# First layer's channel gate: four modulation slabs on VectorE in place of TensorE

## The chip, the cores and the metric

The kernel runs on one core of a Trainium2 chip. TensorE (PE in the profile) multiplies matrices into PSUM, VectorE (DVE) and ScalarE (ACT) work on rows of 128 partitions, GpSimd (POOL) does elementwise work between SBUF tiles, and SyncE (SP) issues the DMAs. The metric is the device time of one execution in microseconds. The kernel before takes 2351.58 us, the median of three runs (2349.04 to 2352.13).

## The reference

Two layers work on 512 latent and 256 context tokens of width 1024. Each layer has a token-mixing part (a convolution branch and differential attention, merged by gates, then one output projection) and a channel part (a squared-ReLU MLP of width 4096, called mixing below, with weights `w_mlp1` and `w_mlp2`). Both parts are modulated by vectors computed from a condition:

```
mx = silu(c) @ w_ada[i] + b_ada[i]            # for the latent tokens
mc = silu(c_ctx) @ w_ada[i] + b_ada[i]        # for the context tokens
shift1, scale1, gate1, shift2, scale2, gate2 = split(mx, 6)     # and the same of mc
h = rmsnorm(x, norm1_g) * (1 + scale1) + shift1
x = x + gate1 * token_mixing(h)
h = rmsnorm(x, norm2_g) * (1 + scale2) + shift2
x = x + gate2 * (square(relu(h @ w_mlp1)) @ w_mlp2)
```

`w_ada[i]` is 1024 by 6144. In the first layer both token groups go through all of this; in the last layer only the latent tokens do. Only the last value in the list, `gate2` of the first layer, is touched by the change. It is first used when the products with `w_mlp2` are added to `x`.

## The kernel before, in words

**Numbers.** Almost every product is made of three: each operand is split into a high half (rounded, made on ScalarE, L76) and a low half (the rest, made on VectorE or GpSimd, L77), and `mm3` adds high by high, high by low and low by high (L109 to L111). A block is 24 such products into one PSUM bank, 512 latent columns wide, or 256 wide for the context tokens and for halves of the latent tokens. Latent blocks have two banks (`mm_tile`), the others two (`mc`). Weights are loaded in slabs of 1 MB through `load_slab` into a ring of two raw tiles and split there; within the first layer's mixing part the low halves are made on GpSimd.

**Slabs.** The modulation weights of a layer are cut into 24 slabs of 256 columns, four for each of the six vectors. Slabs 20 to 23 are `gate2`. There are two ways to work on a slab.

`ada_slab` (L217) uses TensorE: it loads the slab through the raw ring (L81), runs eight products in plain float32 with the two condition vectors as weights (L224; the profile shows 16 instructions), copies the result on ScalarE (L230), makes two transposes on TensorE (L233), and on VectorE two reductions and an addition (L236, L239). The first layer's 24 slabs all go this way: eight at the start, eight among the merge gates, four in the attention output projection (products `ya`) and slabs 20 to 23 in the conv output projection (products `yc`, L1114 and L1115).

`ada_rows` (L245) uses VectorE, and does all 24 slabs of the second layer while the first layer's mixing part runs. It is a generator. A step is half a slab: a load of 512 KB into a tile of its own, `araw`, of which there is one (L263), then for four rows of 128 inputs and the two conditions one multiply-add into `adaac` (L279; the very first of each condition is a product on ScalarE, L276). At the end of a step the next half is loaded. The step after a slab's second half begins by closing that slab: a 32 by 32 block transpose (L289) and a reduction (L290) into `adp`. After eight slabs a fold on TensorE (L252, eight instructions) sums over partitions, and an addition on VectorE (L254) writes the values of these slabs.

**What sets the order.** The engines' order is worked out when the program is built, by a scheduler that goes by readiness in a simulated timeline and by program order. An instruction sits in its engine's queue at the place found then; if what it needs is late on the chip, all behind it on that engine waits. A step is taken at a *tick*, a call of `ada_step` (L1219), whose VectorE instructions may not be placed before the last one recorded in `state["done"]`, a residual addition (L1154) or the low half of a hidden value (L1235).

**The order of the work around the change.** In the first layer: `ya` products, then `yc` products with the low half `cl` (L1103) of the convolution's output, then the output projection `o` (`out_slabs` with a norm: four slabs; the first two go over the two latent halves and the context one after another, two blocks for each; the last two go together, for the first latent half, then the second, then the context, and each is followed by `norm2`), then mixing in four chunks `cch`. In a chunk the hidden blocks `f` (w1, four slabs of two blocks for each token group) are followed by the blocks `r` (w2, four slabs, latent m 0 and 1, then context m 0 and 1). The last chunk's `r` blocks go over the halves, as in the output projection, with the next layer's norm behind them.

Ticks before: in the hidden blocks after each latent block but the last of the chunk, which gives 3 in chunk 0 (its first two slabs go over halves and have none) and 7 in each of chunks 1 to 3; in the `r` blocks of chunks 0 to 2 after each latent block, 8 each. That is 3 + 21 + 24 = 48 ticks for 48 steps. After the hidden blocks of chunk 3, `drain` finishes what is left: the last slab's close and the last fold.

Of the kernel before, what the change touches and what calls it, by code (L numbers as in the profile page):

```python
# [14 lines left out]
P = 128  # L15
# [36 lines left out]
def trunk_kernel(  # L52
# [192 lines left out]
    def ada_rows(i, L):  # L245
# [3 lines left out]
        def fold(s0):  # L249
            ps = state["mi"](f"adaps{i}_{s0}")  # L250
            for c_ in range(4):
                nc.tensor.matmul(ps[32 * c_ : 32 * c_ + 32, :32], fold32, part[:, c_],  # L252
                                 start=True, stop=True, tile_position=(0, 32 * c_))
            nc.vector.tensor_tensor(  # L254
                out=L["ad"][:, :, 2 * s0 : 2 * s0 + 16].rearrange("p q (n m) -> p n q m", n=8),
                in0=ps[:, :32].rearrange("p (n q m) -> p n q m", n=8, q=2),
                in1=L["cols"][:, R_BADA + 2 * s0 : R_BADA + 2 * s0 + 16]
                .rearrange("p (n m) -> p n m", n=8).unsqueeze(2).to_broadcast([P, 8, 2, 2]),
                op=ALU.add)

        def load(n):
            r = state["rp"].tile([P, KT // 2, 256], F32, tag="araw", bufs=1, name=f"ar{i}_{n}")
            nc.sync.dma_start(r, rows(w_ada[i], 256 * (n // 2), 256)[:, 4 * (n % 2) : 4 * (n % 2) + 4])  # L263
            return r

        r = load(0)
        for n in range(48):
            s = n // 2
            if n % 2 == 0:
                a = state["tp"].tile([P, 512], F32, tag="t2k", bufs=state["nt"], name=f"adaac{i}_{s}")  # L270
                a = a.rearrange("p (q n) -> p q n", q=2)
            for j in range(4):
                k = 4 * (n % 2) + j
# [8 lines left out]
            if n < 47:  # L282
                r = load(n + 1)
            yield
            if n % 2:
                if s % 8 == 0:
                    part = spool.tile([P, 4, P], F32, tag="dg", bufs=1, name=f"adp{i}_{s}")[:, :, :32]
                b = state["tp"].tile([P, 512], F32, tag="t2k", bufs=state["nt"], name=f"adat{i}_{s}")
                nc.vector.transpose(out=b, in_=a.rearrange("p q n -> p (q n)"))  # L289
                nc.vector.tensor_reduce(  # L290
                    out=part[:, :, 4 * (s % 8) : 4 * (s % 8) + 4].rearrange("p c n -> p n c"),
                    in_=b.rearrange("p (n c r) -> p n c r", n=4, c=4), axis=AX.X, op=ALU.add)
                if s % 8 == 7:
                    fold(s - 7)
# [154 lines left out]
    for i in range(DEPTH):  # L449
# [658 lines left out]
        for s in range(2):  # L1108
# [89 lines left out]

        w1 = {}
# [188 lines left out]
```

## Time and profile before

| | |
|---|---|
| median of three runs | 2351.58 us |
| the profiled execution | 2353.61 us, with a span of 2351.8 us |
| TensorE busy | 2276.6 us, 97% |
| VectorE busy | 1476.0 us, 63% |
| ScalarE busy | 995.2 us, 42% |
| GpSimd busy | 687.3 us, 29% |
| mean granted TensorE clock | 0.988 |

How to read it: times in rows of the timeline are microseconds from the start of the span, then the duration, the engine, the line of the kernel, the instruction, what it writes and from what, and how many were put together in the row; a bracket holds the idle time of the engine before it and what ended that. Rows of the waits give who waited for whom, the sum, the number of times and the longest. A matmul row of TensorE is longer than the distance to the next one, since products are pipelined: the distance between starts is what a product costs.

| place in the first layer | us from the start |
|---|---|
| last `ya` product | 712.37 |
| first `yc` product | 714.45 |
| first `o` product | 751.81 |
| first `r` residual | 901.9 |
| last fold | 1300.8 |

### The profile page before, as it was taken

The page shows a single profiled execution, that of the slowest core. Times are in us where ns is not written, and L with a number is a line of the kernel's source. Part 1 is how long each engine was busy: PE and PEld are TensorE (multiplying, and loading weights), DVE is VectorE, ACT ScalarE, POOL GpSimd, SP SyncE. Part 2 cuts the span into 40 slices and gives each one's busy share as a digit, 9 for nine tenths or more (in the row PEclk, how much of TensorE's full clock was granted, in tenths as well). Part 3 has the DMA queues.
Part 4 walks back from the last instruction along what each step waited for, and adds up shares of the span by engine and source line. Part 5 has one row for each costly group of instructions (what it writes and reads, how often), then busy time and mean ns, then how long its engine had stood idle before and what let it go on. Part 6 is the DMA issues. An engine that isn't in the chain of part 4 may idle for free.

```text
span 2351.8 us, 36393 instructions
## 1 busy us (share of the span) xinstructions
PE 2276.6 (97%) x14626; PEld 2042.8 (87%) x14626; DVE 1476.0 (63%) x2587; ACT 995.2 (42%) x1965; POOL 687.3 (29%) x790
## 2 busy tenths in 40 slices
PE   7999999999999999999999999999899999999999
PEld 6999998888888988888888988999877879888887
DVE  6777776699656455565655465767759966433332
ACT  5556654522332362332415255655542334432432
POOL 1866764100000133232223266757610000000000
PEclk9999999999999999999999999999999999999999
DMA  9111111143535124333343211111114323223222
GB/s 313 57 42 34 44 46 44 46 160 125 180 119 175 51 81 127 115 128 115 113 130 127 89 46 57 44 43 44 61 59 141 112 90 126 90 90 98 99 90 72
DMA packets 222570, 224.76 MB, mean 96 GB/s; under 512 B 6256, under 2 KB 212544, under 8 KB 222272
## 3 DMA queue, kind: packets, MB, share of 16 engines
q1 hardware_dynamic: 222400, 222.43, 29.4%
q8 instruction: 115, 1.88, 0.3%
q14 instruction: 55, 0.45, 0.1%
HBM read 208.73 MB, written 13.67 MB: 95 GB/s over the span
## 4 chain that ended last, share of the span: by engine, by line
PE 83%; DVE 7%; ACT 4%; POOL 2%; DMA 2%; issue 1%; SPq 0%; ACTq 0%; POOLq 0%; DVEq 0%
PE r L109 6%; PE r L110 6%; PE r L111 6%; PE f L110 6%; PE f L109 6%; PE f L111 6%; PE gt L109 3%; PE gt L110 3%; PE gt L111 3%; PE qk L109 2%; PE qk L110 2%; PE qk L111 2%; PE v L109 2%; PE v L110 2%; PE v L111 2%; PE o L109 2%
## 5 line engine op out<-in xcount | busy, mean ns | idle before, releaser
L110 PE MATMUL f<-h2l,h_w 128*128 128x512 f32 (+1 forms) x832 | 284.5, 343 | 1.1 <-POOL h2l L77 1.1
L109 PE MATMUL f<-h2h,h_w 128*128 128x512 f32 (+1 forms) x832 | 282.9, 343 | 2.2 <-ACT h2h L76 1.7
L111 PE MATMUL f<-h2h,l_w 128*128 128x512 f32 (+1 forms) x832 | 283.0, 342 | 0.0
L109 PE MATMUL r<-fh,h_w 128*128 128x512 f32 (+1 forms) x832 | 283.0, 341 | 0.0
L110 PE MATMUL r<-fl,h_w 128*128 128x512 f32 (+1 forms) x832 | 282.9, 340 | 0.0
L111 PE MATMUL r<-fh,l_w 128*128 128x512 f32 (+1 forms) x832 | 282.8, 340 | 0.0
L77 POOL TENSOR_TENSOR l_w<-r_w,h_w 128x1024 fp32r<-128x1024 f32 x64 | 157.8, 2487 | 339.5 <-ACT h_w L76 339.5
L76 ACT ACTIVATE h_w<-r_w 128x1024 fp32r<-128x1024 f32 x128 | 128.6, 1052 | 254.3 <-PE r L110 117.2
L959 DVE SCALAR_TENSOR_TENSOR cacc<-z,cols,cacc 128x783 f32<-128x783 f32 (+1 forms) x240 | 201.2, 891 | 0.3
L279 DVE SCALAR_TENSOR_TENSOR adaac<-ar,cvec,adaac 128x256 f32<-128x256 f32 x336 | 160.8, 541 | 44.6 <-DMA ar<-in_w_ada_dram 22.7
L109 PE MATMUL qk<-h_wqk,h1h 128*128 128x256 f32 x640 | 183.3, 289 | 0.7 <-ACT h1h L76 0.7
L1154 DVE SCALAR_TENSOR_TENSOR X<-r,ad,X 128x512 f32<-128x512 f32 (+1 forms) x104 | 65.1, 625 | 189.0 <-PE r L111 188.8
L110 PE MATMUL qk<-l_wqk,h1h 128*128 128x256 f32 x640 | 180.6, 284 | 0.0
L111 PE MATMUL qk<-h_wqk,h1l 128*128 128x256 f32 x640 | 176.9, 285 | 0.3 <-POOL h1l L77 0.3
L726 DVE TENSOR_REDUCE st<-S 128x1 f32<-128x768 f32 (+1 forms) x160 | 134.7, 846 | 66.8 <-PE S L724 65.3
L109 PEld LDWEIGHTS f<-h2h,h_w 128*128 128x128 f32 x832 | 158.1, 191 | 21.1 <-ACT h2h L76 2.3
L110 PEld LDWEIGHTS f<-h2l,h_w 128*128 128x128 f32 x832 | 159.1, 191 | 19.6 <-POOL h2l L77 1.9
L111 PEld LDWEIGHTS f<-h2h,l_w 128*128 128x128 f32 x832 | 158.8, 191 | 17.7
L111 PEld LDWEIGHTS r<-fh,l_w 128*128 128x128 f32 x832 | 157.7, 190 | 17.7
L109 PEld LDWEIGHTS r<-fh,h_w 128*128 128x128 f32 x832 | 157.7, 190 | 17.4
L110 PEld LDWEIGHTS r<-fl,h_w 128*128 128x128 f32 x832 | 157.8, 190 | 17.2
L1235 DVE TENSOR_TENSOR fl<-fr,fh 128x512 fp32r<-128x512 f32 (+1 forms) x104 | 67.9, 659 | 138.4 <-ACT fr L1234 138.2
(255 smaller groups left out, 6297.7 us busy)
## 6 DMA issues: line engine op xcount, KB each, us to landing
r_w<-in_w_mlp_dram SPq DMA_DIRECT2D x64, 1024.0 KB, 5.4
ada<-in_w_ada_dram SPq DMA_DIRECT2D x24, 1024.0 KB, 6.1
ar<-in_w_ada_dram SPq DMA_DIRECT2D x48, 512.0 KB, 3.5
r_wqk<-in_w_in_dram SPq DMA_DIRECT2D x32, 512.0 KB, 5.1
r_wg<-in_w_in_dram SPq DMA_DIRECT2D x16, 1024.0 KB, 5.9
r_wv<-in_w_in_dram SPq DMA_DIRECT2D x8, 1024.0 KB, 5.2
r_wao<-in_w_attn_out_dram SPq DMA_DIRECT2D x8, 1024.0 KB, 4.8
r_wo<-in_w_out_dram SPq DMA_DIRECT2D x8, 1024.0 KB, 7.3
```

The costliest lines, as they stand in the source:

```text
L76: nc.scalar.activation(out=hi, in_=src, func=AF.Copy)
L77: return (lo_eng or nc.vector).tensor_tensor(out=lo, in0=src, in1=f32(hi), op=ALU.subtract)
L109: nc.tensor.matmul(ps, sh, mh, start=first, stop=False)
L110: nc.tensor.matmul(ps, sh, ml, start=False, stop=False)
L111: nc.tensor.matmul(ps, sl, mh, start=False, stop=last)
L279: nc.vector.scalar_tensor_tensor(out=a[:, q], in0=r[:, j], scalar=cvec[:, k, q : q + 1], in1=a[:, q], op0=ALU.mult, op1=ALU.add)
L726: nc.vector.tensor_reduce(out=st[:, m : m + 1], in_=S[:, :nkey], axis=AX.X, op=ALU.max, negate=True)
L959: nc.vector.scalar_tensor_tensor(out=ca[cc][:, :CV], in0=zt[cc][:, t : t + CV], scalar=wcol, in1=ca[cc][:, :CV], op0=ALU.mult, op1=ALU.add)
L1154: state["done"] = nc.vector.scalar_tensor_tensor(out=X[:, mb, g], in0=ps[:, :W], scalar=gate[:, s, mb : mb + 1], in1=X[:, mb, g], op0=ALU. ...
L1235: state["done"] = nc.vector.tensor_tensor(out=fl[mb][:, g], in0=r[:, :W], in1=f32(fh[mb][:, g]), op=ALU.subtract).ins
```

## The change

Slabs 20 to 23 of the first layer leave `ada_slab` and the conv output projection, and go to the front of the list of `ada_rows`. The generator now takes a list of groups, each a layer, a first slab and a number of slabs: first four slabs of the first layer, then the second layer's 24 in six groups of four. A fold ends each group, so folds have 16 columns instead of 32 and there are seven instead of three. `adp` has a tile of its own instead of sharing one with the norms.

The list starts earlier. The output projection `o` has four ticks, one after every third block of its first two slabs (the first latter-half block and the last context block in each). Chunk 0 of mixing has two ticks more: after the last latent hidden block, and after the second context block of slab 2. Later ticks stay; those that the new condition adds to the last `r` blocks find the list at its end. That makes 4 + 5 + 21 + 24 = 54 ticks for 56 steps; `drain` takes the last two and the last close and fold.

```diff
-    def ada_rows(i, L):
+    def ada_rows(groups):
+        steps = [(i, s0, ns, n) for i, s0, ns in groups for n in range(2 * ns)]
...
-        def fold(s0):
+        def fold(i, L, s0, ns, part):
             ps = state["mi"](f"adaps{i}_{s0}")
             for c_ in range(4):
-                nc.tensor.matmul(ps[32 * c_ : 32 * c_ + 32, :32], fold32, part[:, c_],
+                nc.tensor.matmul(ps[32 * c_ : 32 * c_ + 32, : 4 * ns], fold32, part[:, c_],
                                  start=True, stop=True, tile_position=(0, 32 * c_))
...
-        r = load(0)
-        for n in range(48):
-            s = n // 2
-            if n % 2 == 0:
+        r = load(steps[0])
+        for at, (i, s0, ns, n) in enumerate(steps):
+            L, s, h = state["mod"][i], n // 2, n % 2
+            if h == 0:
...
-            if n < 47:
-                r = load(n + 1)
+            if at + 1 < len(steps):
+                r = load(steps[at + 1])
             yield
-            if n % 2:
-                if s % 8 == 0:
-                    part = spool.tile([P, 4, P], F32, tag="dg", bufs=1, name=f"adp{i}_{s}")[:, :, :32]
+            if h:
+                if s == 0:
+                    part = spool.tile([P, 4, 4 * ns], F32, tag=f"adp{ns}", bufs=1, name=f"adp{i}_{s0}")
...
-                if s % 8 == 7:
-                    fold(s - 7)
+                if s == ns - 1:
+                    fold(i, L, s0, ns, part)
...
             state["behind"] = ()
-            if not state.get("ada_done"):
-                ada_slab(i, L, 20 + 2 * s)
-                ada_slab(i, L, 21 + 2 * s)
             for m in range(4):
...
                         out_block(w, s, g, m, hidden, gate, nm, norm)
-                        if tick and g is LAT:
+                        if tick and (g is LAT or norm and (6 * s + 2 * halves.index(g) + m) % 3 == 2):
                             tick()
...
+        if not last:
+            rpool = tc.tile_pool(name="araw", bufs=1, reuse_waits="tile")
+            state["rp"] = rpool.__enter__()
+            state["mod"] = {i: L}
+            ada_todo = ada_rows([(i, 20, 4)] + [(i + 1, 4 * n, 4) for n in range(6)])
...
-                  (lambda: mlp1_slab(0, 0), lambda: mlp1_slab(0, 1)))
+                  (lambda: mlp1_slab(0, 0), lambda: mlp1_slab(0, 1)), tick=ada_step)
...
+        late_tick = [(n, 3, 1) for n in range(1, 4)]
...
-                            if g is LAT and (s, m) != (3, 1):
+                            if g is LAT and (cch, s, m) not in late_tick or g is CTXS and (cch, s, m) == (0, 2, 1):
                                 ada_step()
```

More of the change, by code (lines that the diff above doesn't have):

```diff
@@ L259, in fold, with load @@
+                in1=L["cols"][:, R_BADA + 2 * s0 : R_BADA + 2 * (s0 + ns)]
+                .rearrange("p (n m) -> p n m", n=ns).unsqueeze(2).to_broadcast([P, ns, 2, 2]),
                 op=ALU.add)
[L261 to L270 removed]
+        def load(step):
+            i, s0, _, n = step
+            r = state["rp"].tile([P, KT // 2, 256], F32, tag="araw", bufs=1, name=f"ar{i}_{s0}_{n}")
+            nc.sync.dma_start(
+                r, rows(w_ada[i], 256 * (s0 + n // 2), 256)[:, 4 * (n % 2) : 4 * (n % 2) + 4])
+            return r
@@ L1197, in norm2, with ada_step @@
             norm_mod(X, acc, g, int(g.start >= SEQ), L["A2"], sh2, h2h, h2l, f"n2_{i}_{g.start}")
+        if not last:
[3 more added lines that the diff above has]
+            ada_todo = ada_rows([(i, 20, 4)] + [(i + 1, 4 * n, 4) for n in range(6)])
+        def ada_step():
+            if not last:
+                with tc.issue_after(state["done"]):
+                    next(ada_todo, None)
         w1 = {}
```

23 lines of the change are left out of this document (9 added, 14 removed).

## The prediction

> **What bounds the kernel now.** I read the page first, for the share of each engine in the chain of work that ended last, then busy time in four stretches, then PE's waits in the stage where the moved work will run.
>
> ```profile
> PE 83%; DVE 7%; ACT 4%; POOL 2%; DMA 2%; issue 1%; SPq 0%; ACTq 0%; POOLq 0%; DVEq 0%
> ```
>
> The chain is TensorE's for 83% of the span. Whether that holds where the change cuts and where it adds is read from busy time by stretch (columns: PE, weight loads, VectorE, ScalarE, GpSimd, each with its instructions, then TensorE's granted clock):
>
> ```profile
> 700.00:757.00 57.00, 57.00 (x389) 48.96 (x388) 43.67 (x98) 21.15 (x40) 0.00 (x0) 1.00 0.47 153
> 757.00:800.00 43.00, 43.00 (x361) 43.00 (x360) 16.94 (x32) 10.85 (x22) 0.00 (x0) 1.00 0.39 129
> 860.00:905.00 45.00, 45.00 (x257) 39.69 (x256) 21.86 (x42) 21.49 (x40) 18.38 (x8) 1.00 0.35 113
> 1300.00:1320.00 20.00, 20.00 (x174) 19.83 (x173) 6.56 (x12) 6.58 (x12) 5.02 (x3) 1.00 0.16 54
> ```
>
> The first stretch holds the conv output projection, where the four slabs leave; the second the output projection, the third the end of the first mixing chunk's w1 products, where they arrive; the fourth the last w2 products, where the tail of the list arrives. PE is busy all the time in each, at clock 1.00, so a PE microsecond removed there is a microsecond of span, and one inserted costs the same. VectorE has 26.1 us free of 43, 23.1 of 45 and 13.4 of 20. From 860 to 1345 us, the mixing stage that already carries 48 half-slab steps on VectorE, PE's waits come to a single row:
>
> ```profile
> PE adaps L252 <- DVE adp L290: 2.3, 1, 2.3
> ```
>
> So 48 such steps cost PE nothing except at one of three folds. That sets what eight more may cost, and says where to look: at the folds.
>
> **What is removed from PE.** Busy time of the slabs' own instructions (same columns) in three short windows, 64 products of `w_ada` in all:
>
> ```profile
> 712.40:714.45 2.05, 1.87 (x32) 0.94 (x32) 0.00 (x0) 0.39 (x1) 1.00 0.00 0
> 723.40:724.10 0.70, 0.62 (x2) 0.14 (x2) 0.00 (x0) 0.00 (x0) 1.00 0.24 50
> 732.50:734.50 2.00, 1.88 (x30) 0.92 (x30) 0.00 (x0) 0.39 (x1) 1.00 0.00 0
> ```
>
> That is 1.87 + 0.62 + 1.88 = 4.37 us. Each slab then has a pair of transposes that cuts into other products:
>
> ```profile
> 743.18 0.40 PE L118 MATMUL yc<-ch,h_wco 128*128 128x512 f32 x1
> 743.41 0.38 PE L233 MATMUL adaps<-cst,adasb 128*128 128x128 f32 x2
> 743.55 0.48 PE L118 MATMUL yc<-ch,l_wco 128*128 128x512 f32 x1
> 743.87 0.39 PE L118 MATMUL yc<-ch,h_wco 128*128 128x512 f32 x1
> ```
>
> Three products that follow each other at 0.23 us would have started at 743.18, 743.41 and 743.64; the third starts at 743.87. So a pair costs 0.23 us, four cost 0.92. The fold below shows that the first 512-wide product after such a group takes 0.34 to the next start instead of 0.23: 0.11 more, three times, 0.33. Removed: 4.37 + 0.92 + 0.33 = **5.6 us**. What stands to come late next is the low half `cl` that the first conv products need:
>
> ```profile
> 713.85 2.89 DVE L1103 TENSOR_TENSOR cl<-cacc,ch 128x512 fp32r<-128x512 f32 x6
> ```
>
> It is ready at 716.74, and the slabs at 712.5 covered 1.87 us of that. Without them PE reaches the products with `cl` earlier, unless it runs the next block's other products first: between 0 and 1.9 us lost. I take 0: a block has eight such products in each token group, some 2.8 us, and two banks of each kind let the next block begin.
>
> The four 1 MB loads leave SP's queue and the two raw slots, so weights come earlier; PE did not wait for them, so this is worth nothing. VectorE and ScalarE lose their small pieces there, beside a busy PE: nothing.
>
> **What is added to PE.** The list of groups turns three folds of 32 columns into seven of 16: one for layer one, six for layer two.
>
> ```profile
> 1014.88 0.39 PE L109 MATMUL f<-h2h,h_w 128*128 128x512 f32 x1
> 1015.20 0.27 PE L252 MATMUL adaps<-adp,fold 128*32 128x32 f32 x8
> 1015.40 0.50 PE L110 MATMUL f<-h2l,h_w 128*128 128x512 f32 x1
> 1015.74 0.39 PE L111 MATMUL f<-h2h,l_w 128*128 128x512 f32 x1
> 1015.97 0.40 PE L109 MATMUL f<-h2h,h_w 128*128 128x512 f32 x1
> ...
> 1161.91 0.27 PE L252 MATMUL adaps<-adp,fold 128*32 128x32 f32 x8 [2.29 <-DVE adp L290]
> ```
>
> From 1014.88 the next product was due at 1015.11 and starts at 1015.40, and is 0.11 slow itself: 0.40 us a fold. Half the columns may make it cheaper, down to the 0.20 between 1015.20 and 1015.40; I take 0.40, the row itself. Four more: **1.6 us**.
>
> **The waits at the folds.** The second fold kept PE waiting 2.3 us. VectorE shows why, by three kinds of place:
>
> ```profile
> 957.95 0.70 DVE L289 STREAM_TRANSPOSE adat<-adaac 128x512 f32<-128x512 f32 x1
> 958.69 0.69 DVE L290 TENSOR_REDUCE adp<-adat 128x16 f32<-128x512 f32 x1
> ...
> 1036.24 0.70 DVE L289 STREAM_TRANSPOSE adat<-adaac 128x512 f32<-128x512 f32 x1
> 1036.86 0.84 DVE L279 SCALAR_TENSOR_TENSOR adaac<-ar,cvec,adaac 128x256 f32<-128x256 f32 x2
> ...
> 1156.69 0.69 DVE L289 STREAM_TRANSPOSE adat<-adaac 128x512 f32<-128x512 f32 x1
> 1160.28 0.88 DVE L279 SCALAR_TENSOR_TENSOR adaac<-ar,cvec,adaac 128x256 f32<-128x256 f32 x2 [2.90 <-ACT adaac L276]
> ```
>
> These are slabs 4, 8 and 15. The reduction follows the transpose at once; or behind two multiply-adds of the next slab; or behind two that wait 2.90 us for ScalarE's first product of a slab still arriving, and PE with it. Only slabs 13, 14 and 15 of 24 are of the last kind: the place makes it, not the slab. Now count ticks. Before, three are used before the first w2 products; after, four in the output projection and five in the w1 products, nine; every later tick stands where it stood. So the list is six steps on, that is three slabs, four of which are layer one's: where slab n of layer two is transposed now, slab n-1 will be. The folds of slabs 3, 7, 11, 15 and 19 fall on the places of 4, 8, 12, 16 and 20, none of the waiting kind; the last one comes in the drain with no slab behind it. If the order on VectorE stays as it is there, the 2.3 us go too: **-2.3 us**. The nearest rows bound the seven waits at 0 and 7 x 2.3 = 16.1 us. I take half a wait, 1.2 us, for layer one's fold alone, which has no place in the old trace.
>
> **What is added beside PE.** A step on the first half of a slab is six multiply-adds on VectorE (and two products on ScalarE), on the second half eight:
>
> ```profile
> 871.79 2.46 DVE L279 SCALAR_TENSOR_TENSOR adaac<-ar,cvec,adaac 128x256 f32<-128x256 f32 x6
> ...
> 1292.28 3.25 DVE L279 SCALAR_TENSOR_TENSOR adaac<-ar,cvec,adaac 128x256 f32<-128x256 f32 x8
> ```
>
> They take 0.41 us each. Four slabs take 4 x 14 x 0.41 + 4 x (0.70 + 0.69) = 28.5 us of VectorE. Half of it, some 14 us, meets 26.1 free in the output projection; the rest comes in the w1 stretch, where three old steps already ran and five now will; the drain's last slab, 14 x 0.41 + 1.39 = 7.1 us, meets 13.4 free. The steps use one raw tile:
>
> ```profile
> ar<-in_w_ada_dram SPq DMA_DIRECT2D x48, 512.0 KB, 3.5
> ```
>
> so a step takes at least 3.5 + 3.25 = 6.8 us, and the five ticks of the w1 products, some 5 us apart, run ahead of it: the first of them is where the old list has its first, so four steps and a transpose end near 871.8 + 2.5 + 3 x 6.8 + 1.4 = 896. The gate's first user is this row's first start:
>
> ```profile
> L1154 DVE SCALAR_TENSOR_TENSOR X<-r,ad,X x48: 471/617/752, 901.9 to 1234.3; 128x512 f32<-128x512 f32 x24, 128x256 f32<-128x256 f32 x24
> ```
>
> 901.9 leaves 5 us, and a late residual only holds one of two latent banks that is not wanted for another block or two. Nothing. A load of this kind on SP waits for the tile; a weight load behind it is held for a step at most. What can bite in the output projection is `wo`'s last slab, split on VectorE right after the fourth tick:
>
> ```profile
> 787.66 2.36 DVE L77 TENSOR_TENSOR l_wo<-r_wo,h_wo 128x1024 fp32r<-128x1024 f32 x2 [0.48 <-ACT h_wo L76]
> ...
> 796.53 0.48 DVE L1154 SCALAR_TENSOR_TENSOR X<-o,ad,X 128x256 f32<-128x256 f32 x1 [2.76 <-PE o L111]
> ```
>
> Its first block ends by 796.5. It has 24 products of 0.12 (361 of them in the 43.00 us of the second stretch), 2.9 us, so it starts near 793.5. A step of 3.25 in front moves the split's end from 790.0 to 793.3, with a transpose and reduction 794.7: 0 to 1.2 us. I take 0.1, since half the slab is enough to begin.
>
> **Sum.** -5.6 + 1.6 - 2.3 + 1.2 + 0.1 = -5.0 us. On the profiled execution's 2353.61 that is 2348.6; it stood 2.03 above the median of the three runs, 2351.58, from which I forecast 2346.6. 0.2% is 4.7 us, about what a measurement can tell, so this is just beyond it.
>
> **A rule against the change.** GpSimd and VectorE get in each other's way here:
>
> ```profile
> 1131.12 4.94 POOL L77 TENSOR_TENSOR l_w<-r_w,h_w 128x1024 fp32r<-128x1024 f32 x2 [11.47 <-ACT h_w L76]
> ```
>
> ```profile
> 1131.26 5.09 DVE L279 SCALAR_TENSOR_TENSOR adaac<-ar,cvec,adaac 128x256 f32<-128x256 f32 x2 [3.02 <-DMA ar<-in_w_ada_dram]
> ```
>
> Two multiply-adds take 5.09 us beside two splits, not 0.82. The Trainium skill ("SBUF — State Buffer", section "Who interferes with whom") has it that a VectorE instruction with two SBUF inputs contends with a GpSimd instruction that reads SBUF, the later one being blocked outright; this row agrees. By that rule the time would be that of the first rival below; by the waits row, where 48 steps beside the same splits cost PE 2.3 us in all, the sum stays.
>
> **Rivals.** *Held VectorE, no measurable gain.* Between 860 and 905 GpSimd is busy 18.38 us, which leaves 26.6 for two-input work. VectorE's 21.86 plus two more steps and two transposes, 6.5 + 2.8, makes 31.2: layer one's fold could be 4.6 us late, with PE waiting. With that in place of my 1.2, -5.0 - 1.2 + 4.6 = -1.6, 2350.0. For it: the 5.09 row. Against: the fold's place on PE is set when the program is built, and two of the three old folds were placed late enough. One or two waits elsewhere end at the same place: -2.7 or -0.4.
>
> *Slower.* The waiting kind of place is the rule, not the exception, because shorter groups leave the reduction behind the next slab's multiply-adds: all seven folds wait 2.3. Then -5.6 + 1.6 - 2.3 + 16.1 = +9.8, 2361.4. It is slower by over 4.7 from five waits on: -6.3 + 11.5 = +5.2. For it: three neighbouring slabs of 24 show the wait. Against: 21 don't.
>
> *The gain is not all given.* If the `cl` wait and the split both come, -5.0 + 1.9 + 1.1 = -2.0, 2349.6.
>
> **How the numbers follow.** The forecast, folds clear or half a wait, has 0.46; the held VectorE and one to four waits 0.28; the uncovered `cl` or split 0.12; slower 0.10; a larger gain, with no wait at all (-6.3) and cheaper folds (seven at 0.20 save 1.4 more, -7.7), 0.04. Faster is 0.46 + 0.04 = 0.50, same 0.28 + 0.12 = 0.40, slower 0.10. The range goes from -7.7, 2343.9, to three waits, -6.3 + 6.9 = +0.6, 2352.2; the runs shown differ from their median by 0.5 to 2.5, and the order on every engine is made anew, so I open it to 2343 and 2354. The likeliest case alone is 2344.5 to 2347.
>
> **What would show it.** In the changed profile: no PE products of `ada` after 700 us but those of layer one's earlier slabs; PE's time from the last `ya` product to the first `o` product shorter by 5.6; seven groups of L252's successor at 0.4 us; PE's waits for `adp` at 0 to 1 times; output projection as long as before; the last transposes in the last w2 stretch. Wrong if `adp` waits come three times or more, if PE shows a wait at `yc` for `cl` or at `o` for `l_wo`, or if the two joints with the norms come out differently by more than 2 us.

## The result, and the profile after

The changed kernel takes 2380.43 us, the median of four runs (2377.79 to 2383.36), the kernel before 2351.83 beside it (2349.04 to 2352.13). The ratio is 1.0119, with a 95% interval of 1.0104 to 1.0133: 28.6 us slower, where 5 us faster was forecast. The profiled execution took 2383.36 us with a span of 2381.6, which is 29.8 more than before.

The chain that ended last, by engine, from the page of the changed kernel; in the kernel before, TensorE had 83%, VectorE 7% and DMA 2% of it:

```profile
PE 76%; DVE 12%; DMA 5%; ACT 3%; POOL 3%; issue 1%; SPq 0%; ACTq 0%; DVEq 0%; POOLq 0%
```

Busy time by stretch, the same four stretches and columns as in the prediction:

```profile
700.00:757.00 57.00, 57.00 (x358) 51.30 (x357) 45.10 (x91) 20.98 (x40) 0.00 (x0) 1.00 0.33 110
757.00:800.00 43.00, 43.00 (x360) 43.00 (x360) 30.10 (x70) 12.66 (x24) 0.00 (x0) 1.00 0.47 151
860.00:905.00 45.00, 40.27 (x231) 34.65 (x230) 28.31 (x44) 19.76 (x35) 15.00 (x7) 0.96 0.35 114
1300.00:1320.00 20.00, 19.04 (x122) 17.20 (x121) 13.60 (x21) 8.63 (x16) 5.13 (x2) 1.00 0.39 127
```

The first two rows are as forecast. TensorE has no gap where the slabs left (none of its rows there is a product with `w_ada`). The last `ya` product comes at 713.72 in place of 712.37 and the first `o` product at 747.58 in place of 751.81, so the stretch between them has shrunk from 39.4 to 33.9 us, the 5.6 that were forecast. In the output projection VectorE works 30.10 us in place of 16.94 while TensorE stays at 43.00 of 43.00. The third row is where it goes wrong: TensorE works 40.27 of 45.00. VectorE is busy 28.31 us there and free 16.7, so its sum of work is not what stops TensorE.

TensorE's waits from 860 to 1345 us (who waited for what: sum, times, longest); of the kernel before, the one row of 2.3 us stood here:

```profile
PE r L109 <- DVE X L1157: 8.9, 3, 7.2
PE adaps L254 <- DVE adp L296: 8.5, 2, 6.5
PE r L110 <- DVE fl L1243: 5.5, 3, 2.7
```

VectorE is now late for everything it does for TensorE: residuals, folds and low halves `fl`. GpSimd's splits of the weights (L77) serve as marks to see when. Against the kernel before they start 3.0 us earlier at 855 us, 8.8 later at 923 (922.95 against 914.13), 17.5 to 17.9 later from 1065 to 1132, 14.0 later from 1183 to 1249 (the fold that waited 2.3 us before does not wait now), and 26.2 later at the end of the mixing part (1363.19 against 1337.04). Another 3.6 come in the second layer, where nothing is changed. Nearly all is lost in two places: in and just behind the `r` blocks of chunk 0, and at the end of chunk 3.

What goes on there is seen in the timeline of three engines. After, VectorE, over one slab of the list (start, duration; the bracket is the idle time before and what ended it):

```profile
921.56 0.88 DVE L284 SCALAR_TENSOR_TENSOR adaac<-ar,cvec,adaac 128x256 f32<-128x256 f32 x2 [2.78 <-ACT adaac L281]
922.36 0.48 DVE L1157 SCALAR_TENSOR_TENSOR X<-r,ad,X 128x256 f32<-128x256 f32 x1
922.75 5.94 DVE L284 SCALAR_TENSOR_TENSOR adaac<-ar,cvec,adaac 128x256 f32<-128x256 f32 x4
928.62 0.74 DVE L1157 SCALAR_TENSOR_TENSOR X<-r,ad,X 128x512 f32<-128x512 f32 x1
932.47 3.26 DVE L284 SCALAR_TENSOR_TENSOR adaac<-ar,cvec,adaac 128x256 f32<-128x256 f32 x8 [3.11 <-DMA ar<-in_w_ada_dram]
935.64 0.75 DVE L1157 SCALAR_TENSOR_TENSOR X<-r,ad,X 128x512 f32<-128x512 f32 x1
...
939.83 1.28 DVE L284 SCALAR_TENSOR_TENSOR adaac<-ar,cvec,adaac 128x256 f32<-128x256 f32 x3 [2.09 <-ACT adaac L281]
```

GpSimd and ScalarE in the same time:

```profile
922.95 5.07 POOL L77 TENSOR_TENSOR l_w<-r_w,h_w 128x1024 fp32r<-128x1024 f32 x2 [23.55 <-ACT h_w L76]
941.22 4.93 POOL L77 TENSOR_TENSOR l_w<-r_w,h_w 128x1024 fp32r<-128x1024 f32 x2 [13.20 <-ACT h_w L76]
```

```profile
921.01 0.91 ACT L281 ACTIVATE adaac<-ar,cvec 128x256 f32<-128x256 f32 x2 [13.32 <-DMA ar<-in_w_ada_dram]
921.83 1.99 ACT L76 ACTIVATE h_w<-r_w 128x1024 fp32r<-128x1024 f32 x2
939.28 0.91 ACT L281 ACTIVATE adaac<-ar,cvec 128x256 f32<-128x256 f32 x2 [15.46 <-DMA ar<-in_w_ada_dram]
```

Four multiply-adds take 5.94 us, from just before GpSimd's two splits (5.07 us) to just behind them; alone they take 1.6 (the eight at 932.47 take 3.26). They are held. Then VectorE waits 3.11 us for the next load, which could not start while the one raw tile was in use, and 2.09 for the one after. A pair of steps, that is a slab of the list, takes 939.83 - 921.56 = 18.3 us. TensorE needs 16.7 for a w2 slab. Without the hold the pair would take, by an estimate from these rows, 18.3 - (5.94 - 1.6) = 13.9. A pair that meets a split, ends late and so meets the next is called the lock below.

The kernel before, in the same `r` blocks, VectorE and then GpSimd:

```profile
910.84 1.28 DVE L279 SCALAR_TENSOR_TENSOR adaac<-ar,cvec,adaac 128x256 f32<-128x256 f32 x3 [1.44 <-ACT adaac L276]
912.04 0.48 DVE L1154 SCALAR_TENSOR_TENSOR X<-r,ad,X 128x256 f32<-128x256 f32 x1
912.43 1.26 DVE L279 SCALAR_TENSOR_TENSOR adaac<-ar,cvec,adaac 128x256 f32<-128x256 f32 x3
913.62 0.48 DVE L1154 SCALAR_TENSOR_TENSOR X<-r,ad,X 128x256 f32<-128x256 f32 x1
918.52 0.75 DVE L1154 SCALAR_TENSOR_TENSOR X<-r,ad,X 128x512 f32<-128x512 f32 x1 [4.43 <-PE r L111]
919.19 3.24 DVE L279 SCALAR_TENSOR_TENSOR adaac<-ar,cvec,adaac 128x256 f32<-128x256 f32 x8
```

```profile
914.13 4.75 POOL L77 TENSOR_TENSOR l_w<-r_w,h_w 128x1024 fp32r<-128x1024 f32 x2 [11.45 <-ACT h_w L76]
```

Here the split lies from 914.13 to 918.88, in the gap in which VectorE has done its step and waits 4.43 us for TensorE's next block. The next step stands behind that residual, so it cannot start before 919.19. As long as VectorE is ahead of TensorE, its ticks keep the steps clear of the splits; once it is behind, a step starts whenever its load lands, and meets them.

### The profile page after: what moved, and what is told of

Its sections match the earlier page's. It is cut to its first block, busy times and chain, and to the rows that moved or that the text cites. A ratio compares the mean times of both kernels' runs of the same rounds, so it can differ in the third digit from the quotient of the medians.

```text
span 2381.6 us, 36393 instructions
## 1 busy us (share of the span) xinstructions
PE 2285.7 (96%) x14586; PEld 2048.9 (86%) x14586; DVE 1541.8 (65%) x2643; ACT 991.9 (42%) x1967; POOL 685.9 (29%) x790
## 4 chain that ended last, share of the span: by engine, by line
PE 76%; DVE 12%; DMA 5%; ACT 3%; POOL 3%; issue 1%; SPq 0%; ACTq 0%; DVEq 0%; POOLq 0%
PE r L110 5%; PE r L109 5%; PE r L111 5%; DVE adaac L284 5%; PE f L110 4%; PE f L109 4%; PE f L111 4%; DMA ar<-in_w_ada_dram 4%; PE gt L109 3%; PE gt L111 3%; PE gt L110 3%; PE qk L109 2%; PE qk L110 2%; PE qk L111 2%; PE v L109 2%; PE yc L118 2%
## 5 line engine op out<-in xcount | busy, mean ns | idle before, releaser
L284 DVE SCALAR_TENSOR_TENSOR adaac<-ar,cvec,adaac 128x256 f32<-128x256 f32 x392 | 229.4, 646 | 96.1 <-DMA ar<-in_w_ada_dram 54.4
L77 POOL TENSOR_TENSOR l_w<-r_w,h_w 128x1024 fp32r<-128x1024 f32 x64 | 158.5, 2496 | 369.3 <-ACT h_w L76 369.3
L735 ACT ACTIVATE e<-S,st 128x768 f32<-128x768 f32 (+1 forms) x160 | 130.7, 820 | 33.5 <-DVE st L732 33.4
```

Of the source, the lines that this page charges most:

```text
L77: return (lo_eng or nc.vector).tensor_tensor(out=lo, in0=src, in1=f32(hi), op=ALU.subtract)
L284: nc.vector.scalar_tensor_tensor(out=a[:, q], in0=r[:, j], scalar=cvec[:, k, q : q + 1], in1=a[:, q], op0=ALU.mult, op1=ALU.add)
L735: nc.scalar.activation(out=e[:, :nkey], in_=S[:, :nkey], func=AF.Exp, bias=st[:, m : m + 1], accum_out=st[:, 2 + m : 3 + m])
```

## The experiments

**How the loss is counted.** In an undisturbed stretch products of 512 columns start 0.229 us apart and those of 256 columns 0.12. The "loss" below is what the distances between TensorE's starts have over that, where it is more than 0.07, summed from the first `f` product of the first layer to GpSimd's split of the last w2 slab. It holds the waits and the slow products behind them. It is 9.5 us before and 38.9 after.

**Two theories at the start.** The crowding theory: five ticks about 5.5 us apart in the first w1 chunk, with steps of 7 us and more, put VectorE behind, and behind it stays, because a pair of steps held by a split is longer than a w2 slab. The rival: the seven folds themselves, at which TensorE waits 8.5 us. Smaller rivals: the removal uncovers something; the drain's ungated steps; a new order of the early stages.

| kernel | median, us | ratio to before [95%] | loss, us |
|---|---|---|---|
| changed | 2380.43 | 1.0119 [1.0104, 1.0133] | 38.9 |
| 1, before, slabs left out | 2343.97 | 0.9961 [0.9946, 0.9975] | 7.8 |
| 2, before, five ticks | 2366.77 | 1.0066 [1.0044, 1.0088] | 18.4 |
| 3, changed, accumulator in PSUM | 2352.68 | 1.0001 [0.9991, 1.0011] | 12.2 |
| 4, changed, half raw tiles | 2353.63 | 0.9996 [0.9985, 1.0006] | 9.5 |
| 5, changed, four folds | 2369.36 | 1.0070 [1.0054, 1.0085] | 27.5 |
| 6, changed, ticks in `o` | 2366.09 | 1.0053 [1.0033, 1.0073] | 24.9 |
| 7, changed, no late ticks | 2412.16 | 1.0243 [1.0222, 1.0264] | 61.0 |
| 8, changed, first product on VectorE | 2370.42 | 1.0077 [1.0064, 1.0091] | 30.9 |
| 9, before, accumulator in PSUM | 2347.97 | 0.9979 [0.9967, 0.9990] | 5.8 |
| 10, before, half raw tiles | 2350.72 | 0.9986 [0.9973, 0.9999] | 6.9 |
| 11, changed, PSUM, four folds | 2352.38 | 0.9991 [0.9974, 1.0008] | 6.6 |
| 12, changed, half tiles, four folds | 2350.44 | 0.9987 [0.9976, 0.9999] | 8.4 |
| 13, changed, all three | 2348.56 | 0.9986 [0.9974, 0.9998] | 7.4 |

The kernel before had medians of 2353.94, 2353.46, 2352.73 and 2352.64 us beside these.

### 1. The slabs left out

```
-            if not state.get("ada_done"):
-                ada_slab(i, L, 20 + 2 * s)
-                ada_slab(i, L, 21 + 2 * s)
+            if not state.get("ada_done") and s == 0:
+                for q in range(2):
+                    nc.vector.tensor_copy(L["ad"][:, q, 40:48], L["cols"][:, R_BADA + 40 : R_BADA + 48])
```

> The kernel before, with layer one's last four slabs simply left out: the channel mixing gate of layer one is the bias alone, so this leaves out a product. It prices the removal by itself. If the removal gives what the prediction counted (5.6 us of TensorE), the time is 2346 us. If the removal only uncovers the low half cl or the split of l_wo, it is 2350 or more. If the loss in the changed kernel comes from a new order of the early stages, it shows here too, with over 2352.

2343.97 us. The first `o` product's row gives its first start:

```profile
L109 PE MATMUL o<-mh,h_wo x320: 274/283/468, 746.2 to 1976.9; 128*128 128x256 f32 x160
```

746.2 against 751.8: the 5.6 us of the prediction, to a tenth, and TensorE has no wait there. The whole kernel is 10.0 us faster, more than was expected: in the profiled executions 1.7 us come from a smaller loss and 3.0 from the second layer, in which nothing was left out. The removal is not where the loss comes from.

### 2. The crowding alone

```
-                            if g is LAT and (s, m) != (3, 1):
+                            if g is LAT and ((s, m) != (3, 1) or cch == 0) or g is CTXS and (cch, s, m) == (0, 2, 1):
```

> The kernel before, with nothing moved to VectorE, but with five ticks in the first w1 chunk where it has three: the same 48 steps, begun two steps earlier per slab of the first chunk, the accumulator in SBUF and one raw tile. It does alone the part of the change that the crowding theory blames. If crowding alone throws the steps into the GpSimd splits, the w2 period or the period of a pair of steps goes from 16.7 to about 18.4 us in the first chunk and TensorE loses 10 to 20 us there: 2362 to 2372 us. If it takes the eight added steps, that is the sum of VectorE's work, nothing changes: 2349 to 2355.

2366.77 us, 14 more than before, with no work moved at all. VectorE and GpSimd in the first `r` blocks:

```profile
917.27 6.34 DVE L279 SCALAR_TENSOR_TENSOR adaac<-ar,cvec,adaac 128x256 f32<-128x256 f32 x5
...
927.54 3.25 DVE L279 SCALAR_TENSOR_TENSOR adaac<-ar,cvec,adaac 128x256 f32<-128x256 f32 x8 [3.27 <-DMA ar<-in_w_ada_dram]
```

```profile
917.87 5.07 POOL L77 TENSOR_TENSOR l_w<-r_w,h_w 128x1024 fp32r<-128x1024 f32 x2 [15.85 <-ACT h_w L76]
936.36 4.94 POOL L77 TENSOR_TENSOR l_w<-r_w,h_w 128x1024 fp32r<-128x1024 f32 x2 [13.43 <-ACT h_w L76]
```

These are the rows of the changed kernel over again: held for 6.34 us, then 3.27 for the load, splits 18.5 us apart. Two more ticks in one chunk are enough to start the lock; the eight added steps are not needed for it. By the medians that is half of the changed kernel's 28.6 us; in the profiled executions the added loss is 8.9 of 29.4 us, and none of it lies at the end of chunk 3. What the longer list adds, there and in chunk 0, this run does not show.

### 3. The accumulator in PSUM

```
-                a = state["tp"].tile([P, 512], F32, tag="t2k", bufs=state["nt"],
-                                     name=f"adaac{i}_{s0 + s}")
+                a = state["mi"](f"adaac{i}_{s0 + s}")
```

> The changed kernel with the accumulator of the multiply-adds in a PSUM bank in place of SBUF, so that each multiply-add reads one SBUF operand, not two; same ticks, same folds. Crowding theory with contention as its cause: beside a GpSimd split a pair of multiply-adds takes under 1.5 us in place of 5, a step of eight about 3.5 us in place of 4 to 7.5, the w2 period in the first chunk goes from 18.4 to 16.7 us and TensorE's waits of 22.9 us in the mixing stage to under 8: 2352 to 2362 us. If it is the one raw tile and not the contention (3.5 us of load, then the step), the period stays over 17.5 and the time is over 2370. If the folds are the cause, they still wait 8.5 us: over 2370.

2352.68 us: the whole loss is back. VectorE beside a split, then the split:

```profile
927.95 1.54 DVE L283 SCALAR_TENSOR_TENSOR adaac<-ar,cvec,adaac 128x256 f32<-128x256 f32 x3 [3.00 <-DMA ar<-in_w_ada_dram]
929.40 0.48 DVE L1156 SCALAR_TENSOR_TENSOR X<-r,ad,X 128x256 f32<-128x256 f32 x1
929.79 2.06 DVE L283 SCALAR_TENSOR_TENSOR adaac<-ar,cvec,adaac 128x256 f32<-128x256 f32 x4
```

```profile
927.70 4.76 POOL L77 TENSOR_TENSOR l_w<-r_w,h_w 128x1024 fp32r<-128x1024 f32 x2 [11.60 <-ACT h_w L76]
```

Seven multiply-adds run while GpSimd splits, at 0.51 us each, and are not held. They are not faster in themselves: undisturbed, eight take 4.16 us with the accumulator in PSUM and 3.26 with it in SBUF. So what came back is the hold alone. The splits here are 16.4 and 16.7 us apart again (19.2 and 18.8 once each later). The Trainium skill ("SBUF — State Buffer", section "Who interferes with whom") has it that a VectorE instruction with at most one SBUF input does not contend with GpSimd (it excepts the two-port modes); these rows agree. TensorE still lost 2.3 us at one fold and 2.6 at one `fl`.

### 4. Half raw tiles

```
-            r = state["rp"].tile([P, KT // 2, 256], F32, tag="araw", bufs=1, name=f"ar{i}_{s0}_{n}")
-            nc.sync.dma_start(
-                r, rows(w_ada[i], 256 * (s0 + n // 2), 256)[:, 4 * (n % 2) : 4 * (n % 2) + 4])
-            return r
+            rr = []
+            for u in range(2):
+                r = state["rp"].tile([P, KT // 4, 256], F32, tag="araw", bufs=2, name=f"ar{i}_{s0}_{n}_{u}")
+                k0 = 4 * (n % 2) + 2 * u
+                nc.sync.dma_start(r, rows(w_ada[i], 256 * (s0 + n // 2), 256)[:, k0 : k0 + 2])
+                rr += [r[:, 0], r[:, 1]]
+            return rr
```

> The changed kernel with a step's raw tile as two tiles of half the size, so that the next step's first half loads while this step's second half is used. A step waits 2.8 to 3.2 us for its load after the step before; with halves about 1.6. A pair of steps then takes 15 to 16 us in place of 18.3 even when a GpSimd split holds it for 5 us, under the 16.7 of a w2 slab. If the one raw tile is half of the cause, TensorE's losses in the mixing stage (32.6 us in the changed kernel, waits and half-clock products together) come down to 10 to 18: 2356 to 2366 us. If the held multiply-adds alone decide, they stay: over 2374.

2353.63 us: again all of it, more than expected. The group of the multiply-adds (busy, mean ns of one, idle before and what ended most of it), first of the changed kernel, then of this one:

```profile
L284 DVE SCALAR_TENSOR_TENSOR adaac<-ar,cvec,adaac 128x256 f32<-128x256 f32 x392 | 229.4, 646 | 96.1 <-DMA ar<-in_w_ada_dram 54.4
```

```profile
L287 DVE SCALAR_TENSOR_TENSOR adaac<-ar,cvec,adaac 128x256 f32<-128x256 f32 x392 | 174.4, 501 | 10.8 <-DMA ar<-in_w_ada_dram 5.5
```

The idle time falls from 96.1 to 10.8 us, and with it the time in which instructions are held: the mean goes from 646 to 501 ns, though the accumulator is in SBUF as before. VectorE gets ahead again, waits for TensorE (4.98 us before a residual at 931.8), and its steps stay behind the splits. So it takes both, held multiply-adds and one raw tile. Either alone is harmless. The drain is that of the changed kernel in this experiment and in the third, and TensorE loses about 1 us at the end of chunk 3 in place of 11.9, so the drain by itself is not the cause.

### 5. Four folds

```
-            ada_todo = ada_rows([(i, 20, 4)] + [(i + 1, 4 * n, 4) for n in range(6)])
+            ada_todo = ada_rows([(i, 20, 4)] + [(i + 1, 8 * n, 8) for n in range(3)])
```

(`adp` of the groups of eight takes the tile that it has in the kernel before.)

> The changed kernel with layer two's 24 slabs in three groups of eight again: four folds in place of seven. Rival (the folds are the loss): the 8.5 us that TensorE waits at folds come down to about 2, and three folds of 0.4 us go, so 2372 us or less. Crowding theory (five steps about 5.5 us apart in the first w1 chunk, each 7 to 11 us long, put VectorE behind for good): the waits only move from the folds to residuals and low halves, 2376 to 2381 us, and the w2 slabs of the first chunk keep their period of 18.4 us.

2369.36 us, which taken as a number speaks for the rival. The trace does not. Up to 1055 us TensorE loses 20.6 us in the `r` blocks of chunk 0 and the `f` blocks behind them, in the changed kernel 20.0: the waits at folds went from 8.5 to 1.7 us, but a single low half `fl` now waits 7.0, and the splits are 18.2 to 18.8 us apart, as in the changed kernel. The gain, 13.8 us between the two spans, comes from elsewhere: 2.2 lie before 855 us, and the 11.9 that the changed kernel loses from 1317 to 1340 are not lost here. In and behind the `r` blocks of chunk 0, then, a fold is one of the places where TensorE can feel that VectorE is late, no cause of it.

At the end of chunk 3 the traces differ from one load on. The first row is the changed kernel's, the second this one's:

```profile
1266.24 5.56 DVE L284 SCALAR_TENSOR_TENSOR adaac<-ar,cvec,adaac 128x256 f32<-128x256 f32 x3
1262.96 1.26 DVE L284 SCALAR_TENSOR_TENSOR adaac<-ar,cvec,adaac 128x256 f32<-128x256 f32 x3
```

The load before these takes 4.5 us to land in the changed kernel (issued at 1259.60) and 3.4 here (at 1257.36). So the three multiply-adds start 0.17 us before a split there and are held, and 0.81 before it here, and are not. From that split on, the changed kernel's splits are 18.2 to 23.5 us apart again up to 1346 us. Why the load took longer stays open, and with it whether the number of folds has a part in it: experiments 6 and 8, with seven folds, also lose at this place; experiments 3 and 4, with seven folds but out of the lock, do not.

### 6. Six ticks in the output projection, three in the first chunk

```
-                        if tick and (g is LAT or norm and (6 * s + 2 * halves.index(g) + m) % 3 == 2):
+                        if tick and (g is LAT or norm and (2 * halves.index(g) + m) % 2 == 1):
...
-        late_tick = [(n, 3, 1) for n in range(1, 4)]
+        late_tick = [(n, 3, 1) for n in range(4)]
...
-                            if g is LAT and (cch, s, m) not in late_tick or g is CTXS and (cch, s, m) == (0, 2, 1):
+                            if g is LAT and (cch, s, m) not in late_tick:
```

> The changed kernel with six ticks in the output projection and three in the first w1 chunk, where it has four and five: the first w1 chunk is as thin as before the change, everything else as changed (seven folds). Crowding theory: the w2 slabs of the first chunk keep 16.7 us, TensorE's waits there (about 14 us up to 980 us) go: 2358 to 2368 us, what is left being the drain and the second layer. If the folds are the cause, nothing changes by more than 3 us: 2377 to 2383. If VectorE is simply short of time in the whole stage, the loss moves to the output projection: o longer by some us and the total as changed.

2366.09 us. The splits of the first w2 slabs are 16.4 to 17.0 us apart, and TensorE loses nothing there, with the same seven folds. But the crowd has moved: 13.4 us are lost between 825 and 864, where it was 4.8 before: steps stand in front of the additions to `acc` for the norm, and these in turn meet GpSimd's splits (one takes 2.0 us, two take 4.0, in place of 0.4 each). Another 10.6 us are lost at the end of chunk 3, as in the changed kernel. Both the first and the third expectation are partly right.

### 7. No late ticks

```
-        late_tick = [(n, 3, 1) for n in range(1, 4)]
+        late_tick = []
```

> The changed kernel with the three ticks left out at the ends of w1 chunks 1 to 3 given back: 57 ticks for 56 steps, nothing left for the drain. In the changed kernel the waits of 0.5 and 7.2 us for the residual at the drain, with the half-clock products behind them, cost 10.6 us. If the drain's two ungated steps are their cause, these go: 2368 to 2372 us. If VectorE is late there because pairs of steps take 18.3 us against 16.7 for a w2 slab, whatever the drain does, the waits stay and the time is 2377 to 2383.

2412.16 us: both expectations missed, by 29 us and more. The group of the multiply-adds, and the largest of TensorE's waits from 860 to 1345 us:

```profile
L284 DVE SCALAR_TENSOR_TENSOR adaac<-ar,cvec,adaac 128x256 f32<-128x256 f32 x392 | 268.9, 748 | 136.8 <-DMA ar<-in_w_ada_dram 76.3
```

```profile
PE adaps L254 <- DVE adp L296: 25.2, 6, 6.8
```

The splits stay 18.3 to 19.3 us apart (once 20.4) up to 1332 us, where the changed kernel had 16.7 to 17.0 from 1065 to 1249 us. A missing tick at the end of a chunk is a step's time in which VectorE catches up. I had taken the late ticks for a way to fit 56 steps; they are what ends the lock. The pair's 18.3 us against 16.7 holds for as long as the ticks keep coming.

### 8. The first product on VectorE

The accumulator's first product stands on ScalarE ahead of the weight's high half `h_w` (921.01 and 921.83 above), and GpSimd's split follows that; after 921.56 and after 939.83 it starts 1.39 us later both times. It looked as if ScalarE's queue tied the split to the step.

```
-                        nc.scalar.activation(out=a[:, q], in_=r[:, j], func=AF.Copy,
-                                             scale=cvec[:, k, q : q + 1])
+                        nc.vector.tensor_scalar(out=a[:, q], in0=r[:, j], scalar1=cvec[:, k, q : q + 1],
+                                                scalar2=None, op0=ALU.mult)
```

> The changed kernel with the first product of each slab and condition on VectorE in place of ScalarE; accumulator in SBUF, one raw tile, same ticks, seven folds. In the changed kernel ScalarE's first product waits 13 to 15 us for its load, and the weight slab's high half stands right behind it on ScalarE, so that GpSimd's split starts 1.4 us after each slab's first multiply-add and holds the step every time. If that order on ScalarE is a link of the lock, the split comes loose from the steps: their pair no longer takes 18.3 us slab after slab, TensorE's loss in the mixing stage (38.9 us) comes down below 22 and the time is 2350 to 2364 us. If one raw tile and held multiply-adds are enough by themselves, pairs of 18 us stay and the time is 2374 or more.

2370.42 us, between the two expectations. VectorE and GpSimd:

```profile
926.70 7.52 DVE L284 SCALAR_TENSOR_TENSOR adaac<-ar,cvec,adaac 128x256 f32<-128x256 f32 x8 [3.33 <-DMA ar<-in_w_ada_dram]
```

```profile
927.59 5.17 POOL L77 TENSOR_TENSOR l_w<-r_w,h_w 128x1024 fp32r<-128x1024 f32 x2 [11.73 <-ACT h_w L76]
```

The tie is gone (the splits are 16.7, 21.8, 23.5, 18.9 and then 16.7 us apart), and still a step of eight is held for 7.52 us. From the third w1 split (855.07 us in the changed kernel, 849.74 here) to the last w2 split this kernel takes 24 us more than the kernel before, the changed kernel 29. At most 5 of these 29 are the tie's; the two conditions do the rest without it. The rest of the gain lies before that stretch (5.3 us) and in the second layer (3.0). My idea that the tie carries the lock falls.

### 9 and 10. The kernel before, relieved

The edits of 3 and 4 on the kernel before.

> The kernel before with its accumulator in PSUM, so that its 48 steps read one SBUF operand in a multiply-add. It asks whether the kernel before pays anything for the contention. Contention theory: TensorE loses 4.6 us in the mixing stage before, 4.1 of it at one fold; at most this goes: 2347 to 2353 us. If the PSUM accumulator makes the kernel faster by itself, whatever the contention, it is under 2345.

> The kernel before with half raw tiles. It prices what is left of the change when the lock of steps and splits is out of the way: the changed kernel with half raw tiles took as long as the kernel before. If half raw tiles help only against the lock, this is 2347 to 2353 us (the one wait of 2.3 us at a fold, 4.1 us lost with its slow products, may go), and the moved slabs are then worth nothing or less: the same or slower by up to 4 us.

2347.97 and 2350.72 us. The one wait of 2.3 us at a fold goes in both, so it came from the same two conditions. And here is the answer to what the change is worth once the lock is out: 2352.68 with it against 2347.97 without, both with PSUM, and 2353.63 against 2350.72, both with half tiles. The intervals overlap only in the second pair. The change gains nothing in either.

### 11, 12 and 13. Together

The edits of 3 and 5, of 4 and 5, and of all three, on the changed kernel.

> The changed kernel with the accumulator in PSUM and layer two in three groups of eight slabs (four folds). With the accumulator in PSUM alone TensorE still lost 2.3 us at a fold and 2.6 at a low half fl in the mixing stage. If these are chances of the order, this gives 1 to 4 us on it: 2349 to 2352. The removal alone gave 9 us on the kernel before; if nothing is left of the mixing stage's loss, 2346.

> The changed kernel with half raw tiles and four folds in place of seven, accumulator in SBUF. Lock theory: the lock is out, the folds save 3 times 0.4 us and any wait at them: 2349 to 2353 us. If the folds matter by themselves, more: under 2347.

> The changed kernel with all three: accumulator in PSUM, half raw tiles, four folds. Either of the first two was enough against the lock, so both together should give no more than one of them: 2347 to 2353 us. A version faster than both kernels by over 0.2% would be under 2347.

2352.38, 2350.44 and 2348.56 us: the first lies just above its range, the others within theirs. The last one is faster than the changed kernel by 1.3% and than the kernel before by 0.14% [0.02, 0.26]. But the kernel before with the accumulator in PSUM, without the change, has 0.21% [0.10, 0.33]. With PSUM and four folds (experiment 11) the end of the mixing part comes 6.7 us earlier than before, so the removal is kept that far; then the second layer takes 1017.6 us where it took 1014.8. In the profiled executions it took 1015.4 to 1020.5 us in the ten kernels with the longer list, and 1011.8 to 1016.2 in the five without. Nothing in that layer is edited; its order is made anew with every program. Why it mostly comes out longer with the longer list stays open.

## Why the prediction was wrong

**Right.** The 5.6 us of removal (experiment 1). No cover lost at `cl` or `l_wo`: no wait in either place. A fold that doesn't wait costs 0.38 us (at 1126.87 the next product of the same kind is due at 1126.99 and starts at 1127.26, and the one behind it comes 0.11 late), against the 0.40 taken. The fold that waited 2.3 us does not wait any more. The output projection takes its added multiply-adds at no cost to TensorE.

**The step that failed: "five ticks of the w1 products, some 5 us apart, run ahead" of a step of "at least 3.5 + 3.25 = 6.8 us", and "Nothing".** The two numbers said it already: ticks 5 us apart and steps of 6.8. I answered that with the time free until the first residual and let the backlog end there. It doesn't, because a step behind its tick starts when its load lands, not when TensorE's block is done, and so loses what had kept it clear of the splits. The reductions of layer one's last slab end at 904.34 (the last starts at 903.65), where 896 was forecast, and the backlog goes on from there: 18.3 us for a pair against 16.7.

The 6.8 was too small as well, for it has no hold in it. Two of these steps meet a split, one beside the last w1 products and one beside the first w2 products; VectorE first, then GpSimd:

```profile
876.06 7.56 DVE L284 SCALAR_TENSOR_TENSOR adaac<-ar,cvec,adaac 128x256 f32<-128x256 f32 x8 [0.43 <-DMA ar<-in_w_ada_dram]
894.98 5.49 DVE L284 SCALAR_TENSOR_TENSOR adaac<-ar,cvec,adaac 128x256 f32<-128x256 f32 x4 [4.03 <-DMA ar<-in_w_ada_dram]
```

```profile
877.83 5.10 POOL L77 TENSOR_TENSOR l_w<-r_w,h_w 128x1024 fp32r<-128x1024 f32 x2 [10.80 <-ACT h_w L76]
894.49 4.91 POOL L77 TENSOR_TENSOR l_w<-r_w,h_w 128x1024 fp32r<-128x1024 f32 x2 [11.56 <-ACT h_w L76]
```

Eight multiply-adds take 7.56 us in place of 3.25, four take 5.49 in place of 1.6: together 8.2 us, about as much as 904.34 is behind 896. TensorE waits 2.73 us for the low half `fl` behind the four, then 1.99 for the fold. In experiment 3, where nothing is held, these reductions end at 901.89, later than 896 too, but neither wait is there. In all, the term put at "Nothing" came to 38.9 - 9.5 = 29.4 us of loss. "Slower" had a chance of 0.10 in the prediction, but by seven waits at folds, five of which did not come.

**What hid it: free time by sums.** I set 28.5 us of work against 26.1, 23.1 and 13.4 us free. With the same sums VectorE still has 16.7 us free in the 45 us where TensorE waits. What counts is the longest way round through one slab: load, ScalarE, multiply-adds with their hold, load, multiply-adds. Not held, that is 13.9 us, held it is 18.3, and TensorE's 16.7 lies between.

**"Every later tick stands where it stood."** The ticks did. The steps did not, and with them the folds: of the seven, layer one's waited 1.99 us and layer two's first 6.50, neither for the reason of place that I had read from slabs 13 to 15.

**The right row, and the wrong price.** The row of 5.09 us for two multiply-adds beside two splits stood in the prediction, with the rule, and it is the mechanism: experiments 2 and 3 show it. But I priced it as a single delay at layer one's fold, 4.6 us and only a rival. There it came out close, at waits of 2.73 and 1.99 us, but it did not end there. As a period it is 1.6 us in each w2 slab until TensorE waits. The argument against it, that 48 steps beside the same splits cost only 2.3 us, was true of steps that their ticks kept away from the splits.

**The price of a wait.** I counted the old fold's wait as 2.3. With the slow products behind it, it cost TensorE 4.1 in the kernel before, and the slower rival's seven waits of 2.3 were too cheap by the same token.

## What to carry to other kernels

Work that is put beside a busy engine in steps has a period: add up one round through its buffers, with the load that a single buffer keeps back and with what holds it on a shared resource, and compare it with the period of the engine that it must keep up with. Free time summed over a stretch says nothing about that. Where background steps are spaced by ticks, look for what the ticks keep apart (here multiply-adds and splits), and leave a gap now and then in which a backlog can run off.

## What the runs showed of the hardware

A wait of TensorE costs more than itself from some length on. TensorE after its waits in the changed kernel, and the granted clock in this stretch (0.66; columns as above):

```profile
901.13 0.51 PE L110 MATMUL r<-fl,h_w 128*128 128x512 f32 x1 [2.73 <-DVE fl L1243]
901.47 0.60 PE L111 MATMUL r<-fh,l_w 128*128 128x512 f32 x1
901.86 0.63 PE L109 MATMUL r<-fh,h_w 128*128 128x512 f32 x1
904.49 0.31 PE L254 MATMUL adaps<-adp,fold 128*32 128x16 f32 x8 [1.99 <-DVE adp L296]
904.73 0.80 PE L110 MATMUL r<-fl,h_w 128*128 128x512 f32 x1
905.32 0.63 PE L111 MATMUL r<-fh,l_w 128*128 128x512 f32 x1
905.75 0.63 PE L109 MATMUL r<-fh,h_w 128*128 128x512 f32 x1
...
908.31 0.40 PE L109 MATMUL r<-fh,h_w 128*128 128x512 f32 x1
908.55 0.40 PE L110 MATMUL r<-fl,h_w 128*128 128x512 f32 x1
```

```profile
900.00:910.00 10.00, 6.88 (x27) 5.04 (x28) 7.70 (x19) 1.63 (x4) 0.00 (x0) 0.66 0.17 52
```

Behind the first wait, of 2.73 us, two products already start 0.39 us apart (901.47 and 901.86). Behind the second, from 904.73 to 908.31, they start 0.43 to 0.59 us apart, then 0.23 again; the granted clock of these 10 us is 0.66, and 1.00 in the next 10. The two waits of 4.7 us cost 7.3. It was so before too: behind the old fold's 2.29 us, products of 256 columns start 0.21 apart from 1162.6 to 1166.0 in place of 0.12. Waits of 1.85 us (the changed kernel at 1051.92) and 2.02 (experiment 3, at its fold) had no slow products behind them. The Trainium skill ("TensorE: Matmul & The Clock Gate", section "Part 1: The HAM clock gate (the "warmup" mystery)") gives half rate until about 3.4 us of work have passed; the 3.4 to 3.6 us here agree. It puts an idle window of about 3.4 us ahead of that; here 2.29 us were enough.

A multiply-add with its accumulator in PSUM is slower by itself (0.52 us against 0.41 for 128 by 256) and yet the better choice beside GpSimd's splits.
